# Two ends of a feed-forward pipeline: the last two weight groups summed by token halves, and two inner tiles begun on the first half alone

## The chip, the core and the metric

One NeuronCore of a Trainium2 chip runs the whole program. Its engines take instructions from queues of their own, in the order in which these were written: TensorE (PE, matmuls; PEld is its weight load), VectorE (DVE), ScalarE (ACT), GpSimd (POOL) and SyncE (SP, which here issues all DMAs). The metric is device microseconds (us) of one execution, the median of three runs.

## The reference

One layer of a streaming encoder on 1024 new frames and 64 sample frames, D = 1024:

```
h = x + 0.5 * post1(SwiGLU_1(pre1(x)))
h = h + post_mix(token_mix(pre_mix(h)))            # latent attention and stick-breaking attention
h = h + 0.5 * post2(SwiGLU_2(pre2(h)));  y = final(h)
SwiGLU(x) = (silu(x @ w_gate) * (x @ w_up)) @ w_down        # inner width 2816
pre1, post1, ..., final: y / sqrt(mean(y * y) + eps) * gain, over the 1024 features of a token
```

The change touches the two ends of this: pre1 with the first tiles of SwiGLU_1, and the last sums of SwiGLU_2 with post2, the residual and the final norm.

## The kernel before

**Layout.** Features lie on the 128 partitions (KT = 8 blocks of 128), tokens on the free axis. Tokens come in two groups: G1 of 576 (worked in halves of 288) and G2 of 512. Every operand is split into a high and a low part (`split`, lines 142 and 143: a cast on ACT, then a difference on DVE), and a product is three matmuls: high·high, high·low, low·high (`steps`).

**Feed-forward.** `ffn` is a generator that yields after each matmul, so that other stages can draw matmuls from it to fill PE. The inner width is 22 tiles of 128. For one tile it loads two units of `w_gate` and two of `w_up` (`unit`: a DMA of 128x512 into `wr`, four buffers; cast to `wh`, difference to `wl`, eight buffers each), and for each token chunk does 24 matmuls into a gate bank and 24 into an up bank (`f`, three PSUM banks), then the activation (lines 364 to 368) and the split into `hh` and `hl`. Four tiles make a group. A group's sum over its tiles with `w_down` (`down`) is issued after the first tile of the next group, and added into `y` on DVE (line 322). The groups are 4, 4, 4, 4, 4 and 2 tiles: tiles 20 and 21 are the last group, and `down_last` sums it. For the last `ffn` (second feed-forward, G2) it does so by token halves of 256.

**The start.** The 576 tokens of G1 are loaded and normed in two halves: eight squares on ACT, eight fp32 matmuls with ones on PE (`rms_pe`), Ln and Exp on ACT, then for each k a product with gain and r on DVE (line 266, into `t`), a cast to `xh` on ACT and a difference to `xl` on DVE. After the first half three matmuls are drawn from the `ffn`; the rest comes after the second half. The `ffn` takes tile 0 with both halves, then tile 1. After that `late` copies cached keys and values (`ks`, `vs`) from DRAM to DRAM, and the tokens of G2 (`p`) are loaded, squared and summed.

**The end.** `last` runs after the last sum: for each token half a norm, the residual (lines 279 and 280), a second norm, and the output (line 1106, two buffers of 256 KB, DMA at 1108).

**What sets the order.** The program is unrolled. A list scheduler then lays the instructions of each engine into one fixed order, by its own estimate of times; a waiting instruction holds all behind it in its queue.

Of the kernel before, what the change touches and what calls it, by code (L numbers as in the profile page):

```python
# [7 lines left out]
F32 = mybir.dt.float32  # L8
F32R = mybir.dt.float32r
AF = mybir.ActivationFunctionType  # L10
# [5 lines left out]
P = 128  # L16
# [37 lines left out]
EARLY = 3  # L54
# [15 lines left out]
class Layer:  # L70
# [232 lines left out]
    def ffn(self, pool, tmp, n, g, xhi, xlo, y, end=None, tail=None):  # L303
        nc, a = self.nc, self.a
        _, T, C = g
        wg, wu, wd = a[f"wg{n}"], a[f"wu{n}"], a[f"wd{n}"]
        pend = []

# [24 lines left out]
        def down_last(part, step, beside):  # L333
            ws = [[self.unit(pool, wd[mi][:, half * 512:half * 512 + 512]) for mi, _, _ in part] for half in range(2)]
            if step:
                order = [(dt, c0, step) for c0 in range(0, T, step) for dt in range(KT)]
            else:
                order = [(dt, c0, C) for dt in range(KT) for c0 in range(0, T, C)]
            for dt, c0, n in order:
                for _ in product(part, ws[dt // H], False, dt, c0, n):  # L340
                    yield True
                next(beside, None)

        for m in range(0, FT, GROUP):
            part = []
            for mi in range(m, min(m + GROUP, FT)):
                if mi == m + 1 and pend:
                    yield from down(pend.pop(0), m == GROUP)
                gw = units(wg[mi])
                uw = units(wu[mi])  # L350
                hh = pool.tile([P, T], F32R, name="hh")
                hl = pool.tile([P, T], F32R, name="hl")
                for c0 in range(0, T, C):
                    cs = slice(c0, c0 + C)
                    pg = self.bank_f()
                    pu = self.bank_f()
                    for ps, ws in ((pg, gw), (pu, uw)):
                        for k in range(KT):
                            wh, wl = ws[k // H]
                            ks = slice(k % H * P, k % H * P + P)  # L360
                            yield from self.steps(ps[:, :C], wh[:, ks], wl[:, ks], xhi[:, k, cs], xlo[:, k, cs],
                                                  k == 0, k == KT - 1)
                    s = tmp()[:, :C]
                    nc.scalar.activation(s, pg[:, :C], AF.Exp, scale=-1.0)
                    nc.scalar.activation(s, s, AF.Ln, bias=self.one)
                    nc.scalar.activation(s, s, AF.Exp, scale=-1.0)  # L366
                    nc.vector.tensor_tensor(s, pg[:, :C], s, op=ALU.mult)  # L367
                    nc.vector.tensor_tensor(s, pu[:, :C], s, op=ALU.mult)  # L368
                    self.split(hh[:, cs], hl[:, cs], x=s)
                part.append((mi, hh, hl))  # L370
            pend.append(part)
# [3 lines left out]
        yield from down_last(pend.pop(0), tail, end)  # L375
# [645 lines left out]
def body(tc, a, ctx):  # L1021
# [58 lines left out]
    def last(gi, y, res, pool, step):  # L1080

        t0, T, C = groups[gi]
        yT = a["yT"].rearrange("(k p) t -> p k t", p=P)
        for c0 in range(0, T, step):
            cs = slice(c0, c0 + step)
            tmp = lambda: pool.tile([P, step], F32, name="t", bufs=4)

            def norm():

                r = pool.tile([P, step], F32, name="r", bufs=4)  # L1090
                if c0 + step == T:
                    L.rms_pe(tmp, L.bank_f, [y[:, k, cs] for k in range(KT)], step, r)
                else:
                    for k in range(KT):
                        L.square(tmp, r, y[:, k, cs], k == 0)
                    L.rsqrt(L.bank_f, r, step, D, r)
                return r

            r = norm()
            for k in range(KT):  # L1100
                L.residual(res[:, k, cs], y[:, k, cs], "post2", k, r, None)
            r = norm()
            for k in range(0, KT, 2):
                o = pool.tile([P, 2, step], F32, name="out", bufs=2)
                for i in range(2):
                    nc.vector.scalar_tensor_tensor(o[:, i], y[:, k + i, cs], L.gain("final", k + i), r,
                                                   op0=ALU.mult, op1=ALU.mult)
                nc.sync.dma_start(yT[:, k:k + 2, t0 + c0:t0 + c0 + step], o)
# [17 lines left out]
    with tc.tile_pool(name="x0", bufs=1) as xp:  # L1126
# [4 lines left out]
        zero = L.ffn(F, fact, 1, G1, *x0, y0)  # L1131
        for c0 in (0, half):
# [6 lines left out]
            r = xp.tile([P, half], F32, name="r", bufs=2)  # L1139
            L.rms_pe(tmp, L.bank_f, [y[:, k, cs] for k in range(KT)], half, r)  # L1140
            L.at_r = 0.0
            L.scaled(tmp, lambda k: y[:, k, cs], "pre1", r, x0[0][:, :, cs], x0[1][:, :, cs], pace=False)

            if c0 == 0:
                for _ in range(EARLY):
                    next(zero)
# [167 lines left out]
```

## Time and profile before

| | us |
|---|---|
| median of three runs (2336.8 to 2340.3) | 2339.42 |
| the profiled execution, whole | 2337.27 |
| its span in the trace | 2335.5 |
| PE busy | 2256.7 (97%) |
| DVE busy | 1429.8 (61%) |
| ACT busy | 1287.3 (55%) |

PE is busy almost throughout; its slices of the span read 7 tenths in the first and 5 tenths in the last. A busy matmul counts from its start to its modelled end, so neighbours overlap; the rate is read from starts. A row of the timeline reads: start, busy us, engine, line, operation, output<-inputs, size, count, and in brackets the idle time before it and what ended it.

### The profile page before, as it was taken

What the parts mean: (1) busy time and instruction counts of PE and PEld (TensorE: products, weight loads), DVE (VectorE), ACT (ScalarE), POOL (GpSimd) and SP (SyncE); (2) the same over time, 40 slices, a digit from 0 to 9 for tenths busy, and PEclk for the clock granted to TensorE, in tenths of its full rate; (3) what the DMA queues carried; (4) which work ended last, traced back from release to release, by engine and by line L of the source; (5) the groups of instructions that cost most, each with busy time, mean ns of one, the idle gap of its engine ahead of it and who ended that gap; (6) DMA issues with size and microseconds to landing.
All of it is one profiled execution on the core that took longest, in us unless ns stands there. A gap on an engine that the chain in (4) does not pass through costs nothing.

```text
span 2335.5 us, 37504 instructions
## 1 busy us (share of the span) xinstructions
PE 2256.7 (97%) x13841; PEld 2034.3 (87%) x13841; DVE 1429.8 (61%) x2528; ACT 1287.3 (55%) x2494; POOL 32.9 (1%) x224
## 2 busy tenths in 40 slices
PE   7999999999999999999999999999999999999995
PEld 7999999989987877779888998999899898888884
DVE  5444444674348778755874377878777488444445
ACT  6443334463257878663553478777777445433333
POOL 0000000000000000000000000000000000000000
PEclk9999999999999999999999999999999999999998
DMA  6332222453454434343555532323222434333321
GB/s 211 102 96 81 84 78 86 143 183 119 167 155 128 139 98 128 108 140 99 162 159 181 162 96 88 102 73 100 73 73 70 135 106 147 121 96 96 98 86 36
DMA packets 186615, 268.80 MB, mean 115 GB/s; under 512 B 59216, under 2 KB 68048, under 8 KB 186400
## 3 DMA queue, kind: packets, MB, share of 16 engines
q1 hardware_dynamic: 186432, 266.41, 37.1%
q8 instruction: 109, 1.79, 0.3%
q14 instruction: 74, 0.61, 0.1%
HBM read 227.61 MB, written 40.88 MB: 115 GB/s over the span
## 4 chain that ended last, share of the span: by engine, by line
PE 73%; DVE 10%; ACT 8%; DMA 5%; issue 3%; SPq 1%; DVEq 0%; POOL 0%; ACTq 0%; POOLq 0%
PE f L157 50%; PE s L157 9%; PE t L157 6%; PE v L157 6%; DVE a L620 2%; PE t L161 2%; ACT a L615 1%; ACT a L614 1%; DVE a L617 1%; ACT a L616 1%; DMA e<-h 1%; DVE wl L143 1%; DVE pl L687 1%; DVE y L280 1%; ACT wh L142 1%
## 5 line engine op out<-in xcount | busy, mean ns | idle before, releaser
L157 PE MATMUL f<-xh,wh 128*128 128x288 f32 (+1 forms) x2112 | 695.2, 330 | 9.5 <-ACT xh L142 7.2
L157 PE MATMUL f<-xh,wl 128*128 128x288 f32 (+1 forms) x2112 | 695.9, 330 | 0.0
L157 PE MATMUL f<-xl,wh 128*128 128x288 f32 (+1 forms) x2112 | 694.9, 329 | 0.8 <-DVE xl L143 0.8
L142 ACT CAST wh<-wr 128x512 fp32r<-128x512 f32 x638 | 384.5, 619 | 495.7 <-PE f L157 341.0
L143 DVE TENSOR_TENSOR wl<-wr,wh 128x512 fp32r<-128x512 f32 x638 | 429.5, 688 | 246.6 <-ACT wh L142 223.8
L157 PEld LDWEIGHTS f<-xh,wh 128*128 128x128 f32 x2112 | 397.9, 189 | 40.1 <-ACT xh L142 8.3
L157 PEld LDWEIGHTS f<-xl,wh 128*128 128x128 f32 x2112 | 398.1, 189 | 29.8 <-DVE xl L143 1.7
L157 PEld LDWEIGHTS f<-xh,wl 128*128 128x128 f32 x2112 | 398.1, 188 | 29.2 <-issue 2.4
L157 PE MATMUL f<-hl,wh 128*128 128x288 f32 (+2 forms) x1072 | 351.6, 328 | 0.1
L157 PE MATMUL f<-hh,wh 128*128 128x288 f32 (+2 forms) x1072 | 349.9, 327 | 0.5 <-DVE y L322 0.3
L157 PE MATMUL f<-hh,wl 128*128 128x288 f32 (+2 forms) x1072 | 349.8, 326 | 0.0
L157 PEld LDWEIGHTS f<-hl,wh 128*128 128x128 f32 x1072 | 202.1, 189 | 14.6 <-issue 1.4
L157 PEld LDWEIGHTS f<-hh,wh 128*128 128x128 f32 x1072 | 201.7, 188 | 14.9 <-DVE y L322 1.3
L157 PEld LDWEIGHTS f<-hh,wl 128*128 128x128 f32 x1072 | 202.0, 188 | 13.9 <-issue 1.2
L322 DVE TENSOR_TENSOR y<-f,y 128x288 f32<-128x288 f32 (+2 forms) x248 | 127.7, 519 | 101.1 <-PE f L157 100.7
L367 DVE TENSOR_TENSOR act<-f,act 128x288 f32<-128x288 f32 (+1 forms) x132 | 70.2, 532 | 120.3 <-ACT act L366 120.0
L368 DVE TENSOR_TENSOR act<-f,act 128x288 f32<-128x288 f32 (+1 forms) x132 | 70.3, 533 | 76.3 <-PE f L157 72.9
L687 DVE TENSOR_TENSOR pl<-t,ph 128x384 fp32r<-128x384 f32 (+1 forms) x160 | 98.3, 631 | 25.0 <-ACT ph L686 23.7
L142 ACT CAST hh<-act 128x288 fp32r<-128x288 f32 (+1 forms) x132 | 65.1, 494 | 77.4 <-DVE act L368 77.1
L157 PE MATMUL v<-pl,v 128*128 128x256 f32 x320 | 89.8, 304 | 18.3 <-DVE pl L687 18.0
L686 ACT CAST ph<-t 128x384 fp32r<-128x384 f32 (+1 forms) x160 | 83.6, 542 | 29.4 <-PE t L161 27.7
L161 PE MATMUL t<-c_ident,a 128*128 128x128 f32 x616 | 90.5, 273 | 2.6 <-ACT a L631 2.6
(308 smaller groups left out, 3409.0 us busy)
## 6 DMA issues: line engine op xcount, KB each, us to landing
wr<-in_wg SPq DMA_DIRECT2D x176, 256.0 KB, 2.9
wr<-in_wu SPq DMA_DIRECT2D x176, 256.0 KB, 3.1
wr<-in_wd SPq DMA_DIRECT2D x176, 256.0 KB, 2.9
wr<-in_win SPq DMA_DIRECT2D x44, 256.0 KB, 3.1
kl<-ks SPq DMA_DIRECT2D x64, 128.0 KB, 2.8
wr<-in_wout SPq DMA_DIRECT2D x32, 256.0 KB, 2.9
h<-y SPq DMA_DIRECT2D x16, 288.0 KB, 2.5
p<-in_xT SPq DMA_DIRECT2D x16, 256.0 KB, 3.4
```

Of the source, the lines that this page charges most:

```text
L142: nc.scalar.copy(hi, x)
L143: nc.vector.tensor_tensor(lo, x, f(hi), op=ALU.subtract)
L157: self.nc.tensor.matmul(out, lhsT=lhsT, rhs=rhs, start=start, stop=stop)
L161: self.nc.tensor.transpose(out, x, ident)
L280: nc.vector.tensor_tensor(y, y, x, op=ALU.add)
L322: nc.vector.tensor_tensor(yy, ps[:, :C], yy, op=ALU.add)
L367: nc.vector.tensor_tensor(s, pg[:, :C], s, op=ALU.mult)
L368: nc.vector.tensor_tensor(s, pu[:, :C], s, op=ALU.mult)
L614: nc.scalar.activation(av, z, AF.Abs)
L620: nc.vector.tensor_tensor_scan(a[:, 0:n - 1][:, ::-1], zs[:, 1:n][:, ::-1], a[:, 0:n - 1][:, ::-1], BIG, op0=ALU.add, op1=ALU.subtract)
L686: nc.scalar.copy(ph[:, end:], tr[:, end:])
L687: nc.vector.tensor_tensor(pl[:, end:], tr[:, end:], f(ph[:, end:]), op=ALU.subtract)
```

## The change

- At the start, the first half's squares are summed on DVE (line 221), and one matmul with ones gives the sum. `ffn` gets `lead`: the first two inner tiles do their 48 matmuls each for the first token half before either does its second half. Matmuls are drawn between the steps of the second half's norm and split.
- At the end, the sum of group 16 to 19 is no longer issued between tiles 20 and 21: `down_last` sums all six tiles, 16 to 21, for the first token half and then for the second, and after every product one step of `last` is issued. `last` is now a generator: first half's norm, residual, second norm and the squares of the second half lie between the products.
- The twelve `w_down` units which this needs at once have room in `spare`: nine lie in the place of the group-1 input `x`, three in `wh` and `wl`. The last `hh` and `hl` lie in another pool. The output buffers are five instead of two (`e`).

```diff
-    def ffn(self, pool, tmp, n, g, xhi, xlo, y, end=None, tail=None):
+    def ffn(self, pool, tmp, n, g, xhi, xlo, y, end=None, tail=None, spare=None, own=None, lead=0):
...
+        def unit(src):
+            if not room:
+                return self.unit(pool, src)
+            hi, lo = room.pop(0)
+            raw = pool.tile([P, 512], F32, name="wr")
+            nc.sync.dma_start(raw, src)
+            self.split(hi, lo, x=raw)
+            return hi, lo
...
+        for c0 in range(0, T, C) if lead else ():
+            for mi in range(lead):
+                if c0 == 0:
+                    ahead.append(open_tile(mi))
+                yield from inner(*ahead[mi], c0)
+        part.extend((t[0], t[3], t[4]) for t in ahead)
         for m in range(0, FT, GROUP):
+            for mi in range(m, min(m + GROUP, FT)):
+                if mi == m + 1 and pend and not (tail and m + GROUP >= FT):
+                    yield from down(pend.pop(0), m == GROUP)
...
+        if spare:
+            room.extend(spare())
-        yield from down_last(pend.pop(0), tail, end)
+        yield from down_last(sum(pend, []), tail, end)
...
+        one, two = slice(0, step), slice(step, T)
+        r1, r2, r3, r4 = row(), row(), row(), row()
+        for k in range(KT):
+            L.square(tmp, r1, y[:, k, one], k == 0)
+            yield
+        ps = None
+        for k in range(KT):
+            if k < KT - 1:
+                L.square(tmp, r3, y[:, k, two], k == 0)
+            if k == 0:
+                L.rsqrt(L.bank_f, r1, step, D, r1)
+            elif k < 5:
+                for i in range(2 * k - 2, 2 * k):
+                    moved(i, one, r1)
+                    L.square(tmp, r2, y[:, i, one], i == 0)
+            elif k == 6:
+                L.rsqrt(L.bank_f, r2, step, D, r2)
+            if k < KT - 1:
+                yield
+        sq = tmp()
+        nc.scalar.activation(sq, y[:, KT - 1, two], AF.Square)
...
+        scale(ps, r3)
+        for k in range(0, KT, 2):
+            out(k, one, r2)
+        for k in range(KT):
+            moved(k, two, r3)
+        L.rms_pe(tmp, L.bank_f, [y[:, k, two] for k in range(KT)], step, r4)
+        for k in range(0, KT, 2):
+            out(k, two, r4)
...
-        zero = L.ffn(F, fact, 1, G1, *x0, y0)
+        zero = L.ffn(F, fact, 1, G1, *x0, y0, lead=LEAD)
...
+            if c0 == 0:
+                for k in range(KT):
+                    L.square(tmp, r, y[:, k, cs], k == 0)
+                L.rsqrt(L.bank_f, r, half, D, r)
+                L.scaled(tmp, lambda k: y[:, k, cs], "pre1", r, x0[0][:, :, cs], x0[1][:, :, cs], pace=False)
+                for _ in range(3 * KT):
+                    next(zero)
+                continue
             L.rms_pe(tmp, L.bank_f, [y[:, k, cs] for k in range(KT)], half, r)
-            if c0 == 0:
-                for _ in range(EARLY):
+            for _ in range(3 * KT):
+                next(zero)
+            for k in range(KT):
+                L.scaled(tmp, lambda k: y[:, k, cs], "pre1", r, x0[0][:, :, cs], x0[1][:, :, cs], ks=[k], pace=False)
+                for _ in range((LEAD - 1) * 6 if k < KT - 1 else 0):
                     next(zero)
```

What this does to the queues is seen at three places. SP at the start of the program, first before, then after the change (`ks` and `vs` are the DRAM copies, `p` the tokens of G2, `wr` weights):

```order
L299 DMA wr<-in_wu 128x512 x2
L299 DMA wr<-in_wg 128x512
L129 DMA ks_88<-in_c_k 16x16384
L299 DMA wr<-in_wg 128x512
L299 DMA wr<-in_wu 128x512
L130 DMA vs_94<-in_c_v 16x16384
L299 DMA wr<-in_wu 128x512
L1050 DMA p<-in_xT 128x512 x3
```

```order
L299 DMA wr<-in_wg 128x512 x2
L129 DMA ks_88<-in_c_k 16x16384
L130 DMA vs_94<-in_c_v 16x16384
L1081 DMA p<-in_xT 128x512
L299 DMA wr<-in_wu 128x512 x2
L1081 DMA p<-in_xT 128x512 x4
```

The two copies now stand one behind the other, and the first `p` directly behind them.

ACT at the start, where the second token half is cast to `xh`, before and after (`act` is an activation of tile 0 or 1, `hh` its cast):

```order
L142 CAST xh<-t 128x288
L366 ACTIVATE act<-act 128x288
L142 CAST xh<-t 128x288 x5
L217 ACTIVATE p<-p 128x512
L142 CAST wh<-wr 128x512
L142 CAST xh<-t 128x288 x2
L220 ACTIVATE p<-p 128x512
```

```order
L243 ACTIVATE r<-f,eps 128x288
L244 ACTIVATE r<-r 128x288
L142 CAST xh<-t 128x288 x2
L217 ACTIVATE p<-p 128x512
L142 CAST xh<-t 128x288 x2
L142 CAST hh<-act 128x288
L220 ACTIVATE p<-p 128x512
L142 CAST xh<-t 128x288 x3
L374 ACTIVATE act<-f 128x288
L375 ACTIVATE act<-act,ones 128x288
L220 ACTIVATE p<-p 128x512
L142 CAST xh<-t 128x288
```

Before, one square of `p` stands ahead of the last two casts; now one stands ahead of the last six, a second ahead of four and a third ahead of the last.

DVE at the end of the program, from the last sums on, before and after (`y<-f,y` adds a product, lines 279 and 280 are the residual, `r<-r,t` adds squares, 1106 and 1130 are the output):

```order
L322 TENSOR_TENSOR y<-f,y 128x256 x6
L279 SCALAR_TENSOR_TENSOR y<-y,c_gains,r 128x256 x2
L280 TENSOR_TENSOR y<-y,h 128x256 x2
...
L221 TENSOR_TENSOR r<-r,t 128x256 x7
L1106 SCALAR_TENSOR_TENSOR out<-y,c_gains,r 128x256 x8
L279 SCALAR_TENSOR_TENSOR y<-y,c_gains,r 128x256 x2
```

```order
L221 TENSOR_TENSOR r<-r,t 128x256 x3
L279 SCALAR_TENSOR_TENSOR y<-y,c_gains,r 128x256
L334 TENSOR_TENSOR y<-f,y 128x256
L280 TENSOR_TENSOR y<-y,h 128x256
L221 TENSOR_TENSOR r<-r,t 128x256 x2
L334 TENSOR_TENSOR y<-f,y 128x256
L221 TENSOR_TENSOR r<-r,t 128x256
L1130 SCALAR_TENSOR_TENSOR e<-y,c_gains,r 128x256 x3
L334 TENSOR_TENSOR y<-f,y 128x256
L1130 SCALAR_TENSOR_TENSOR e<-y,c_gains,r 128x256 x5
L279 SCALAR_TENSOR_TENSOR y<-y,c_gains,r 128x256 x2
```

The residual and squares of the first half now stand among the sums of the second; the first half's output stands around the last sum.

## Rows read from the trace of the kernel before

**Rows 1.** Stages: length, busy PE, PEld, DVE, ACT, POOL (count), PE clock, DMA share, GB/s.

```profile
13.50:39.70 26.20, 21.00 (x98) 18.03 (x98) 17.97 (x41) 15.94 (x38) 0.00 (x0) 0.80 0.60 197
39.70:80.00 40.30, 40.30 (x307) 40.30 (x306) 21.55 (x40) 22.05 (x46) 0.00 (x0) 1.00 0.41 126
80.00:2255.30 2175.30, 2132.39 (x13150) 1925.17 (x13149) 1342.70 (x2340) 1216.67 (x2342) 32.68 (x220) 1.00 0.38 115
2255.30:2288.00 32.70, 32.70 (x146) 27.09 (x145) 13.34 (x20) 8.18 (x13) 0.00 (x0) 1.00 0.15 47
2301.00:2335.50 34.50, 11.18 (x36) 7.56 (x34) 21.82 (x56) 12.99 (x32) 0.00 (x0) 0.77 0.18 61
```

**Rows 2.** Chain of waits, start of the program: start us, us, what.

```profile
27.28 7.25 DMA p<-in_xT
...
36.07 8.94 PE f L157 x54
```

**Rows 3.** Timeline of ACT, where the second token half is normed and cast.

```profile
26.05 0.45 ACT L244 ACTIVATE r<-r 128x288 f32<-128x288 f32 x1
...
29.76 1.29 ACT L142 CAST xh<-t 128x288 fp32r<-128x288 f32 x3 [0.99 <-DVE t L266]
34.55 0.63 ACT L217 ACTIVATE p<-p 128x512 f32<-128x512 f32 x1 [3.50 <-DMA p<-in_xT]
```

**Rows 4.** Timeline of SP, the two copies from DRAM to DRAM.

```profile
21.11 0.50 SPq L129 DMA_DIRECT2D ks<-in_c_k  x1
...
25.40 0.71 SPq L130 DMA_DIRECT2D vs<-in_c_v  x1
```

**Rows 5.** DMA issues of the first 45 us: count, us from issue to landing.

```profile
ks<-in_c_k SPq DMA_DIRECT2D x1, 8.1
vs<-in_c_v SPq DMA_DIRECT2D x1, 7.8
```

**Rows 6.** Timeline of PE: tile 21, then the last sums, at a steady rate.

```profile
2283.64 0.39 PE L157 MATMUL f<-xh,wl 128*128 128x512 f32 x1
...
2287.72 0.39 PE L157 MATMUL f<-xh,wl 128*128 128x512 f32 x1
...
2293.90 0.28 PE L157 MATMUL f<-hh,wh 128*128 128x256 f32 x1
...
2300.62 0.28 PE L157 MATMUL f<-hh,wl 128*128 128x256 f32 x1
```

**Rows 7.** Chain of waits from the last sum to the end.

```profile
2302.33 0.88 DVE y L279 x2
...
2308.27 0.35 DVE r L221
...
2311.83 6.34 PE f L157 x18
2318.19 0.48 ACT r L243
2319.15 0.88 DVE y L279 x2
```

**Rows 8.** Timeline of DVE in the same stretch.

```profile
2300.22 0.42 DVE L322 TENSOR_TENSOR y<-f,y 128x256 f32<-128x256 f32 x1 [0.29 <-PE f L157]
...
2308.17 3.60 DVE L221 TENSOR_TENSOR r<-r,t 128x256 f32<-128x256 f32 x7
...
2330.63 1.67 DVE L1106 SCALAR_TENSOR_TENSOR out<-y,c_gains,r 128x256 f32<-128x256 f32 x4 [1.51 <-DMA out_yT<-out]
```

**Rows 9.** Timeline of SP: loads of `w_down` ahead of the last two sums.

```profile
2226.74 19.54 SPq L299 DMA_DIRECT2D wr<-in_wd  x8
...
2265.49 2.89 SPq L299 DMA_DIRECT2D wr<-in_wd  x4
```

**Rows 10.** Page: a costly group (count, busy us, mean ns), a DMA issue (us to landing).

```profile
L142 ACT CAST wh<-wr 128x512 fp32r<-128x512 f32 x638 | 384.5, 619 | 495.7 <-PE f L157 341.0
...
wr<-in_wd SPq DMA_DIRECT2D x176, 256.0 KB, 2.9
```

More of the change, by code (lines that the diff above doesn't have):

```diff
@@ L50 @@
 SLACK = 1.15
-EARLY = 3
+LEAD = 2
 EASE = 0.8
@@ L333, in down_last @@
         def down_last(part, step, beside):
[L334 to L340, printed above, removed]
+            ws = [[unit(wd[mi][:, half * 512:half * 512 + 512]) for mi, _, _ in part] for half in range(2)]
@@ L341, in down_last @@
+            order = [(dt, c0) for c0 in range(0, T, step) for dt in range(KT)] if step else \
+                [(dt, c0) for dt in range(KT) for c0 in range(0, T, C)]
+            for dt, c0 in order:
+                for _ in product(part, ws[dt // H], False, dt, c0, step or C):
                     yield True
                 next(beside, None)
-        for m in range(0, FT, GROUP):
-            part = []
[L346 to L371, printed above, removed]
@@ new lines, in open_tile, with inner @@
+        def open_tile(mi):
+            gw = units(wg[mi])
+            uw = units(wu[mi])
+            room = own if own and mi == FT - 1 else pool
+            hh = room.tile([P, T], F32R, name="hh")
+            hl = room.tile([P, T], F32R, name="hl")
+            return mi, gw, uw, hh, hl
+        def inner(mi, gw, uw, hh, hl, c0):
+            cs = slice(c0, c0 + C)
+            pg = self.bank_f()
+            pu = self.bank_f()
+            for ps, ws in ((pg, gw), (pu, uw)):
+                for k in range(KT):
+                    wh, wl = ws[k // H]
+                    ks = slice(k % H * P, k % H * P + P)
+                    yield from self.steps(ps[:, :C], wh[:, ks], wl[:, ks], xhi[:, k, cs], xlo[:, k, cs],
+                                          k == 0, k == KT - 1)
+            s = tmp()[:, :C]
+            nc.scalar.activation(s, pg[:, :C], AF.Exp, scale=-1.0)
+            nc.scalar.activation(s, s, AF.Ln, bias=self.one)
+            nc.scalar.activation(s, s, AF.Exp, scale=-1.0)
+            nc.vector.tensor_tensor(s, pg[:, :C], s, op=ALU.mult)
+            nc.vector.tensor_tensor(s, pu[:, :C], s, op=ALU.mult)
+            self.split(hh[:, cs], hl[:, cs], x=s)
@@ L1078, in finish, with last @@
             t = L.done(t + SLACK * (T / 960 + 0.15))
-    def last(gi, y, res, pool, step):
+    def last(gi, y, res, pool):
         t0, T, C = groups[gi]
+        step = T // 2
         yT = a["yT"].rearrange("(k p) t -> p k t", p=P)
[L1084 to L1108, printed above, removed]
@@ new lines, in last, with scale, moved, out @@
+        tmp = lambda: pool.tile([P, step], F32, name="t", bufs=4)
+        row = lambda: pool.tile([P, step], F32, name="r", bufs=4)
+        def scale(ps, r):
+            nc.scalar.activation(r, ps, AF.Ln, bias=L.eps, scale=1.0 / D)
+            nc.scalar.activation(r, r, AF.Exp, scale=-0.5)
+        def moved(k, cs, r):
+            L.residual(res[:, k, cs], y[:, k, cs], "post2", k, r, None)
+        def out(k, cs, r):
+            o = pool.tile([P, 2, step], F32, name="e", bufs=5)
+            for i in range(2):
+                nc.vector.scalar_tensor_tensor(o[:, i], y[:, k + i, cs], L.gain("final", k + i), r,
+                                               op0=ALU.mult, op1=ALU.mult)
+            nc.sync.dma_start(yT[:, k:k + 2, t0 + cs.start:t0 + cs.stop], o)
@@ new lines, in last @@
+        sq = tmp()
+        nc.scalar.activation(sq, y[:, KT - 1, two], AF.Square)
+        ps = L.bank_f()[:, :step]
+        L.mul(ps, lhsT=L.ones, rhs=r3, start=True, stop=False)
+        L.mul(ps, lhsT=L.ones, rhs=sq, start=False, stop=True)
+        scale(ps, r3)
[6 more added lines that the diff above has]
+            out(k, two, r4)
@@ L1208, in body @@
     x3 = pair(lp, T2, "x")
-    tmp = lambda: lp.tile([P, T2], F32, name="e", bufs=3)
+    tmp = lambda: lp.tile([P, T2], F32, name="e", bufs=5)
     L.wait(L.at_r)
@@ L1218, in body, with spare @@
     y3 = lp.tile([P, KT, T2], F32, name="y")
-    third = L.ffn(F, fact, 2, G2, *x3, y3, tail=T2 // 2)
+    def spare():
+        both = [z.rearrange("p k t -> p (k t)") for z in pair(fp, T1, "x")]
+        return [[z[:, i:i + 512] for z in both] for i in range(0, KT * T1, 512)]
+    third = L.ffn(F, fact, 2, G2, *x3, y3, end=lambda: last(1, y3, h, lp), tail=T2 // 2, spare=spare, own=lp)
     L.filler = third
```

16 lines of the change are left out of this document (13 added, 3 removed).

## The prediction

> **What bounds the kernel now.** I read the table of stages first, since a mean over the span says little here. From 39.7 to 2288 PE is busy without gaps worth the name (40.30 of 40.30, 2132 of 2175, 32.70 of 32.70 [rows 1]); the change leaves the matmuls of that stretch and their order nearly as they were, and I count it as unchanged. Two stretches are not bound by PE: 13.5 to 39.7, where the granted clock is 0.80 and PE has done only 82 matmuls of the feed-forward (98 records less 16 passes of the norm's eight ones matmuls), and 2301.0 to 2335.5, 34.5 us in which the norms of the two token halves run one after the other and PE is busy for 11 [rows 1].
>
> At the start I then read the chain of waits. Its longest link is not the norm but a transfer: `p`, issued at 27.28, lands 7.25 later, and PE resumes at 36.07 [rows 2]. The ACT timeline says why PE cares: a square of `p` sits in ACT's queue ahead of the last two casts of the second token half and holds ACT for 3.50 us [rows 3]. At the end the chain has DVE nearly alone: residual from 2302.33, squares from 2308.27, then eighteen ones passes and the second half's whole tail from 2318.19 [rows 7].
>
> **The change at the end, step by step.** Rates first: 18 steps from 2283.64 to 2287.72 are 0.2267 us per 512-wide matmul, 56 steps from 2293.90 to 2300.62 are 0.120 per 256-wide one [rows 6].
>
> - Both versions are alike up to the end of tile 20's products. Counting back from 2287.95 (2287.72 + 0.23), where the last sums begin, 96 + 48 matmuls of 0.2267 put that at 2255.3.
> - After the change: tile 21, 48 × 0.2267 = 10.9. Then 16 products of six tiles, 288 × 0.120 = 34.6. (The four moved tiles cost 192 × 0.120 − 96 × 0.2267 = 1.3 more in halves.)
> - Tile 21's split must be done before its matmuls. Before, the last sums took 2287.95 to 2300.74 (2300.62 + 0.12) for 96 × 0.12 = 11.5, so 1.3 was lost there. Now five other tiles stand ahead of it in the first product, 1.8 us of work: I take 0.5 (bounds 0 and 1.3).
> - Two ones matmuls for r1 and r2 now stand between products. Nine of them took 6.34 at the end, at a clock of 0.77, so 0.7 each [rows 1, 7]; on a busy PE less: 0.5 each, 1.0 (bounds 0.6 and 1.4).
> - The second ones matmul waits for DVE, with the last product behind it on PE. r1 is ready 0.5 + 0.48 + 0.42 after the tenth product begins, with latencies 1.5 [rows 3, 7]. From there DVE has eight residual pairs (2302.33 to 2308.27, 5.9), twelve adds at 0.35 to 0.51 (the first of the chain; 3.60 for seven), and five sums at 0.42 [rows 7, 8]: 12.2 to 14.1, so done at 13.7 to 15.6. PE gets there after six products, 13.0. A wait of 0.7 to 2.6; I take 1.0, near the lower end, because the adds now alternate between two accumulators instead of chaining on one.
>
> PE is then through at 2255.3 + 10.9 + 34.6 + 0.5 + 1.0 + 1.0 = 2303.3, where before it was at 2301. Behind that hangs one sum (0.42), one square (taken as 0.42 too), a ones matmul (0.5), Ln (0.48) and Exp (0.42, a little under the 0.45 of 288 columns) and some 0.5 of latencies: the second half's residual begins at 2306.1 instead of 2319.15 [rows 3, 7, 8]. From there to the end of the span it was 16.35; 1.5 goes, since the third of the half's four output pieces need no longer wait for a buffer (1.51 [rows 8]), and 14.85 stays. End at 2320.95 instead of 2335.5: **14.5 us saved**. With each bound at its worst (0.8, 0.4, 1.6, and the 1.5 kept) it is 10.2, at its best 16.4. What the first half's squares, residual and output cost DVE and ACT is hidden by the second half's 17.3 us of matmuls (144 × 0.12); without that cover they would cost the 17 us that they cost now.
>
> Here a page of the Trainium skill would say otherwise. In the steady row 256 columns take 0.120 [rows 6]. "TensorE: Matmul & The Clock Gate", section "Back-to-back issue gap", gives N/2.4 + 2.5 ns, 109 ns for 256 columns. By it the 288 matmuls are an estimated 31.4 and the end comes 3 us sooner; the row is this very stream, so I stay with it.
>
> **The change at the start.** At 39.70 PE has done 82 of the 192 matmuls of tiles 0 and 1 and goes on at 40.3/307 = 0.131 each [rows 1], so 120 are done at 44.7. After the change these 120 are: both tiles for the first half (96), and tile 0's gate for the second.
>
> - First half: its norm loses seven ones matmuls on PE and gains seven adds on DVE; but the weight casts now stand ahead of Ln on ACT. I count nothing for it (−0.5 to +1). The second half's r is ready at 26.5 [rows 3]; now, with two more units of weights split earlier, I take 25 (bounds 24 and 26.5).
> - PE's 72 matmuls behind the second half's ones cover 72 × 0.131 = 9.5 us; the ones end a Ln and an Exp before r, at 24, so to about 33.5. The sixth cast ended at 31.05, 4.5 after r [rows 3]; eight at that pace are through by 31, PE would not wait at all, and 120 would be done at 33.5 + 24 × 0.131 = 36.7: 8.0 saved. That is one bound.
> - But ACT's queue has the first `p` square after two casts, the second after four, the third before the eighth. `p` now follows both copies directly on SP. `ks` landed at 21.1 + 8.1 = 29.2, `vs` at 25.4 + 7.8 = 33.2, `p` behind it at 34.5 [rows 2, 4, 5]. With `ks` issued at about 20.8 (the weights ahead of it are split a little earlier than for the 21.1), `vs` at its heels and `p` at 22, `p` lands no earlier than 22 + 7.25 = 29.3 and no later than 28.9 + 4.0 + 1.3 = 34.2. I take 33, nearer the later end, since the row of `p` had only the rest of one copy ahead of it.
> - From 33: square 0.63, two casts, `hh`, the second `p` (about 35), square, three casts that wait for DVE products, two activations, third square, last cast at 39, and two adds of `p` on DVE ahead of its difference: tile 0's second gate ends at about 40, 4.7 before the 44.7. In pieces it keeps PE half idle, so the lower clock may last some us past it, as in the stage with 0.80 before; I take off 0.5. **4.2 us saved**, bounds 0 and 8.0.
>
> The second place for the skill: the row shows `p` 7.25 us underway with one copy in front. "DMA: Bandwidth & Descriptors", section "Queues, rings and completion order", says that an SDMA engine consumes descriptors in ring order, so `p` would wait for all of both copies. By that rule the landing is near 34 and the gain 3.2; by the flat 7.25 it is near 29 and the gain about 7.
>
> **Sum.** 2337.27 − 14.5 − 4.2 = 2318.6 for the profiled execution; it lay 2.15 under the median, so 2320.7 against 2339.42. I say 2320.5.
>
> **Rivals.**
>
> - *Late `p` (0.15).* The start gives nothing: `p` lands at 38 or later, or the third one does, and ACT sits ahead of the casts as before. For it: the 3.50 us wait that is there already, and three squares instead of one among the casts. Against it: 9.5 us of matmuls that need none of this. 2337.27 − 14.5 + 2.15 = 2324.9.
> - *Early `p` (0.08).* It lands near 29 and the casts are never held: 8.0 at the start, some 15 at the end: 2316.4.
> - *DVE bounds the second half (0.10).* Adds at 0.51 and each switch between sums, squares and residual paying its latency: PE waits 2.6 or more before the last product, the end gives 10.2: 2337.27 − 10.2 − 4.2 + 2.15 = 2325.0. For it: DVE is already at 21.8 of 34.5 in the tail [rows 1], and its work is now pressed beside the sums.
> - *The weights come late (0.04; the other side).* Place: the first product over six tiles, which needs six units, and the fifth, which needs the other six; all twelve pass SP, ACT and DVE during tiles 20 and 21, 21.8 us. Four units took 2.89, 0.72 each; eight took 19.54, 2.44 each, but those waited for PE to free `wh` [rows 9], which nine of the twelve need not. At 0.72 they are hidden; at 2.44, 29.3, they come 7.5 late and the time is 2328. It is slower than before from (21.8 + 18.7)/12 = 3.4 us per unit. If each went its round alone (2.9 to landing, 0.62 for the cast [rows 10], as much for the difference: 4.1), 49.2 − 21.8 = 27.4 are lost and the time is 2348. Against it: four buffers keep loads in flight, and DMA is at 0.15 there [rows 1].
>
> **How the numbers follow.** My forecast, 2317 to 2324, has 0.62; with the rivals 0.99, and 0.01 is for what I did not think of. The range 2313 to 2328 holds the first three rivals and leaves out the last one's far end. 0.2%, 4.7 us, is about what a measurement here can tell from no change. Faster than that needs more than 4.7 of the 18.7: all cases but the late weights, 0.94. Within it 0.02, slower 0.04.
>
> **What would show it.** In the trace after: sums of 256 columns at 0.120 without gaps to about 2299 of a span near 2317, less than 20 us from the last of them to the end; one wait of about 1 us of PE for DVE before the last product; no wait for `w_down`; residual of the second half beginning some 15 us before the end. At the start ACT waiting for `p` between the second and third cast of the second half, PE pausing after about 33 and running on at about 40. Wrong if PE pauses in the sums for a weight or a bank, if the tail is over 22 us, or if `p` lands before 30 or after 36.

## The result: 1.05% faster, and the profile after

Median of four runs each: 2339.84 us before (2336.8 to 2340.3), 2315.18 after (2311.39 to 2316.89); ratio 0.9895, 95% interval 0.9878 to 0.9912, so between 20.6 and 28.5 us are saved. The forecast was 2320.5 (2313 to 2328): the time lies in that range, but below the 2317 to 2324 to which the forecast gave 0.62 of its chances.

The profiled execution of the changed kernel took 2316.89, with a span of 2315.1: 20.4 us shorter than the span of before. The medians lie 24.7 apart because the one execution is 2.57 under its median and the other 1.71 over it. The longer runs of the changed kernel have the lower granted clock: the two of 2316.9 and 2316.7 had a mean of 0.996, those of 2313.7 and 2311.4 one of 0.998, and 0.002 of 2315 are 4.6 us. So single steps are read below from positions in the trace, not from differences of medians.

The table of stages of the changed kernel answers to [rows 1]; columns as there. The last sums now begin at 2261.34.

```profile
13.50:39.70 26.20, 24.36 (x145) 22.29 (x146) 17.43 (x41) 16.13 (x40) 0.00 (x0) 1.00 0.61 195
39.70:80.00 40.30, 40.30 (x306) 40.30 (x305) 22.18 (x42) 22.63 (x48) 0.00 (x0) 1.00 0.41 132
2261.30:2297.30 36.00, 35.82 (x293) 35.38 (x293) 21.32 (x55) 10.79 (x28) 0.00 (x0) 1.00 0.01 2
2300.30:2315.10 14.80, 5.45 (x16) 3.93 (x16) 9.19 (x24) 3.91 (x11) 0.00 (x0) 0.78 0.32 106
```

At the start 145 records of matmuls stand where there were 98, and the clock reads 1.00 where it was 0.80. The 1.00 does not hold for all of it: from 14 to 17.9 matmuls start 0.24 us apart, the pace of 1.2 GHz, where 0.131 is the pace later. PE's timeline of after:

```profile
17.41 0.44 PE L157 MATMUL f<-xh,wh 128*128 128x288 f32 x1
17.65 0.44 PE L157 MATMUL f<-xl,wh 128*128 128x288 f32 x1
```

Before, there was a second stretch at 0.24, from 36.07 to 39.55, right behind PE's wait of 3.73 us for a cast. In this execution of after there is none. At the end 34.5 us of norms behind the last sum have become 18, the last 14.8 of which are the second half's tail.

**Where the 20.4 us come from.** The same instruction, ACT's first activation of a gate, shows how far the two executions are apart. First the timeline of before, then that of after, at tile 3 and at tile 18 of the last feed-forward.

```profile
77.25 0.40 ACT L364 ACTIVATE act<-f 128x288 f32<-128x288 f32 x1
...
2228.61 0.59 ACT L364 ACTIVATE act<-f 128x512 f32<-128x512 f32 x1
```

```profile
70.86 0.40 ACT L374 ACTIVATE act<-f 128x288 f32<-128x288 f32 x1
...
2223.76 0.59 ACT L374 ACTIVATE act<-f 128x512 f32<-128x512 f32 x1
```

6.4 us are saved by 77 us of the span; 4.85 are left at 2228; so the end saves 20.4 − 4.85 = 15.55, and the middle gave back 1.5. The change has no step of its own there. Three stretches of the middle have a lower granted clock after, and two before; each costs some (1 − 0.83) × 10 = 1.7 us of full clock, so the one more is about the size of the 1.5. But PE's waits there are not the same either (they add up to 42.3 us after and 41.1 before), and between 77 and 2228 the distance goes up to 7.1 and down to 3.8 us. What the 1.5 is made of is not shown. One stretch of after:

```profile
1640.00:1650.00 10.00, 8.81 (x53) 8.52 (x54) 6.98 (x12) 6.75 (x12) 0.44 (x3) 0.83 0.11 42
```

**The start after.** ACT's timeline, where the second half is cast, answers to [rows 3]:

```profile
23.53 0.44 ACT L244 ACTIVATE r<-r 128x288 f32<-128x288 f32 x1
24.56 0.86 ACT L142 CAST xh<-t 128x288 fp32r<-128x288 f32 x2 [0.59 <-DVE t L266]
31.09 0.63 ACT L217 ACTIVATE p<-p 128x512 f32<-128x512 f32 x1 [5.67 <-DMA p<-in_xT]
31.63 0.75 ACT L142 CAST xh<-t 128x288 fp32r<-128x288 f32 x2
...
33.26 0.63 ACT L220 ACTIVATE p<-p 128x512 f32<-128x512 f32 x1 [0.54 <-DMA p<-in_xT]
...
36.34 0.41 ACT L142 CAST xh<-t 128x288 fp32r<-128x288 f32 x1
```

The casts stop for 5.67 us at the first square of `p`, as forecast. SP's timeline and the landings of the two copies (count, us) say why; they answer to [rows 4, 5]:

```profile
19.89 0.50 SPq L129 DMA_DIRECT2D ks<-in_c_k  x1
20.45 0.58 SPq L130 DMA_DIRECT2D vs<-in_c_v  x1
21.07 0.61 SPq L1081 DMA_DIRECT2D p<-in_xT  x1
```

```profile
ks<-in_c_k SPq DMA_DIRECT2D x1, 6.4
vs<-in_c_v SPq DMA_DIRECT2D x1, 8.6
```

`ks` is there at 26.3, `vs` at 29.05, `p` at 31.09. PE's timeline shows what that costs: the 24th, 96th and 120th matmul of tiles 0 and 1 are these, and the last three wait for the last cast.

```profile
19.76 0.29 PE L157 MATMUL f<-xh,wl 128*128 128x288 f32 x1
...
32.14 0.29 PE L157 MATMUL f<-xh,wl 128*128 128x288 f32 x1
...
36.80 0.40 PE L157 MATMUL f<-xh,wh 128*128 128x288 f32 x1 [0.50 <-ACT xh L142]
37.92 0.40 PE L157 MATMUL f<-xl,wh 128*128 128x288 f32 x1 [0.71 <-DVE xl L143]
38.16 0.29 PE L157 MATMUL f<-xh,wl 128*128 128x288 f32 x1
```

The 120 are done at 38.3. Without a pause they would be done at 32.27 + 24 × 0.131 = 35.4, so the pause costs 2.9.

**The end after.** PE's timeline: the first of the last sums, the two ones matmuls between them, the last sum.

```profile
2261.34 0.28 PE L157 MATMUL f<-hh,xh 128*128 128x256 f32 x1
...
2280.93 0.59 PE L157 MATMUL f<-r,ones 128*128 128x256 f32 x2
...
2294.65 0.70 PE L157 MATMUL f<-r,ones 128*128 128x256 f32 x2 [0.18 <-DVE r L221]
...
2297.21 0.28 PE L157 MATMUL f<-hh,wl 128*128 128x256 f32 x1
```

The chain of waits behind it (start, us, what) answers to [rows 7]:

```profile
2297.82 0.34 DVE y L334
...
2298.65 0.71 PE f L157 x2
...
2299.39 0.48 ACT r L1121
...
2300.34 0.88 DVE y L279 x2
...
2307.67 0.48 ACT r L243
...
2309.51 2.38 DVE e L1130 x6
```

No gap stands in the sums but the 0.18 (0.34 from start to start beyond the pitch). The residual of the second half begins 14.76 us before the end.

### The profile page after: what moved, and what is told of

Same layout as the page of the kernel before. It is cut to its first block, busy times and chain, and to the rows that moved or that the text cites. A ratio compares the mean times of both kernels' runs of the same rounds, so it can differ in the third digit from the quotient of the medians.

```text
span 2315.1 us, 37626 instructions
## 1 busy us (share of the span) xinstructions
PE 2246.7 (97%) x13911; PEld 2032.5 (88%) x13911; DVE 1427.7 (62%) x2533; ACT 1285.0 (56%) x2494; POOL 32.9 (1%) x224
## 4 chain that ended last, share of the span: by engine, by line
PE 73%; DVE 10%; ACT 8%; DMA 4%; issue 3%; SPq 1%; DVEq 0%; POOL 0%; ACTq 0%; POOLq 0%
PE f L157 50%; PE s L157 9%; PE t L157 7%; PE v L157 6%; DVE a L651 2%; PE t L161 2%; DVE a L648 1%; ACT a L647 1%; ACT a L646 1%; ACT a L645 1%; DVE pl L718 1%; DVE wl L143 1%; ACT wh L142 1%; DMA tmp<-in_xT 1%; DVE a L657 1%
## 5 line engine op out<-in xcount | busy, mean ns | idle before, releaser
L142 ACT CAST wh<-wr 128x512 fp32r<-128x512 f32 x629 | 378.7, 619 | 467.8 <-PE f L157 309.8
L143 DVE TENSOR_TENSOR wl<-wr,wh 128x512 fp32r<-128x512 f32 x629 | 422.8, 687 | 250.5 <-ACT wh L142 228.2
L157 PEld LDWEIGHTS f<-xh,wl 128*128 128x128 f32 x2112 | 398.5, 189 | 29.3 <-issue 2.4
L157 PE MATMUL f<-hl,wh 128*128 128x288 f32 (+2 forms) x1032 | 336.2, 326 | 0.0
L157 PE MATMUL f<-hh,wh 128*128 128x288 f32 (+2 forms) x1032 | 334.5, 325 | 1.1 <-DVE y L334 1.1
L157 PE MATMUL f<-hh,wl 128*128 128x288 f32 (+2 forms) x1032 | 334.5, 324 | 0.0
L157 PEld LDWEIGHTS f<-hh,wh 128*128 128x128 f32 x1032 | 193.7, 188 | 13.7 <-DVE y L334 1.7
L157 PEld LDWEIGHTS f<-hl,wh 128*128 128x128 f32 x1032 | 193.9, 188 | 12.9 <-issue 1.4
L157 PEld LDWEIGHTS f<-hh,wl 128*128 128x128 f32 x1032 | 193.9, 188 | 12.6 <-issue 1.2
L334 DVE TENSOR_TENSOR y<-f,y 128x288 f32<-128x288 f32 (+2 forms) x240 | 121.9, 512 | 96.5 <-PE f L157 96.1
L718 DVE TENSOR_TENSOR pl<-t,ph 128x384 fp32r<-128x384 f32 (+1 forms) x160 | 98.2, 630 | 24.5 <-ACT ph L717 23.2
```

The source lines that it names most:

```text
L142: nc.scalar.copy(hi, x)
L143: nc.vector.tensor_tensor(lo, x, f(hi), op=ALU.subtract)
L157: self.nc.tensor.matmul(out, lhsT=lhsT, rhs=rhs, start=start, stop=stop)
L334: nc.vector.tensor_tensor(yy, ps[:, :C], yy, op=ALU.add)
L718: nc.vector.tensor_tensor(pl[:, end:], tr[:, end:], f(ph[:, end:]), op=ALU.subtract)
```

## Experiments

All times are medians beside runs of the kernel before on the same chip, there 2338.3 to 2338.4 (13 to 17 runs).

**Start and end apart.** The end alone:

```
-        zero = L.ffn(F, fact, 1, G1, *x0, y0, lead=LEAD)
+        zero = L.ffn(F, fact, 1, G1, *x0, y0)        # and the start loop of before, EARLY = 3
```

> The start of the kernel before with the end of the changed one. Theory A (the two parts are worth what the two traces show, and add up): the end alone saves 15.6 us: tile 21's last matmul to the first ones matmul of r3 36.0 us, the second half's residual 3.0 us after that, 14.8 us from there to the end of the span; 2339.8 - 15.6 = 2324.2 us, between 2322.5 and 2326.5. Theory B (the forecast's own terms for the end were right, and what the changed kernel gained beyond them came from elsewhere): 14.5 us, 2325.3 us, with PE waiting about 1 us for DVE before the last product. Theory C (the start and the end are not independent, a part of the 24.7 us is only there with both): less than 13 us saved, above 2327 us.

Measured: 2321.36 (ratio 0.9932, 0.9916 to 0.9947): 15.9 us by the ratio. The end is worth what it is in the changed kernel: from the first of the last sums (2265.61) to the end of the span (2319.4) it is 53.8, as in the changed kernel (2315.1 − 2261.34 = 53.8). The start alone:

```
-                if mi == m + 1 and pend and not (tail and m + GROUP >= FT):
+                if mi == m + 1 and pend:             # and last(), tail, spare, own as before
```

> The start of the changed kernel with the end of the kernel before. Theory A (parts add up): 120 matmuls of tiles 0 and 1 are done at 38.3 us of the span instead of 44.7, so 6.4 us saved, less what low clock in the middle gives or takes (up to 3 us between runs): 2333.4 us, between 2331 and 2336. Theory B (the forecast's 4.2 us for the start): 2335.6 us. Theory C (the start's gain is lost again in the middle, where other work waits for other things): within 2 us of 2339.8.

Measured: 2333.2 (0.9977, 0.9966 to 0.9988), 5.4 us (2.8 to 8.0); 120 matmuls are done at 39.5. 15.9 and 5.4 make 21.3, inside the interval of the whole change: no sign that the parts depend on each other, and the end is some three quarters of the gain. The median can't tell theory A's 6.4 for the start from theory B's 4.2. The trace is nearer to B: the gate of tile 3 that stands at 77.25 before and at 70.86 after is here at 73.17, so 4.1 are saved by then.

**Cover at the end.**

```
                 for _ in product(part, ws[dt // H], False, dt, c0, step or C):
                     yield True
-                next(beside, None)
```

> The changed kernel, with no step of the norms issued between the products of the last six tiles: all of it comes behind the last sum. Theory A (what saved the time at the end is that the first half's norms lie beside the second half's matmuls): PE is through the sums about 1.4 us sooner, but then residual of the first half 5.9, some fifteen adds at 0.34, a second norm of about 2 and eight outputs of 0.41 stand ahead of the second half's residual, which begins 13.5 us later than in the changed kernel: 2328.7 us (2326 to 2332). Theory B (the gain came from the six-tile sum itself, from the tile order or from the five output buffers): not more than 5 us slower, under 2320 us.

Measured: 2330.76 (0.9968, 0.9957 to 0.9978). PE's timeline shows where the time went, behind the last sum at 2294.72:

```profile
2306.40 1.22 PE L157 MATMUL f<-r,ones 128*128 128x256 f32 x2 [10.97 <-DVE r L221]
```

From the first sum (2260.14) to the second half's residual (2311.79) it is 51.65, in the changed kernel 39.0: 12.65 more, 13.5 expected. Of the 7.5 us that are left by the ratio the start has 5.4, so some 2 are left for the six-tile sum and the five buffers, less than these intervals can show; what saves is that the norms lie beside matmuls.

**DVE's slack there.**

```
+        idle = pool.tile([P, step], F32, name="idle")
...
                     L.square(tmp, r2, y[:, i, one], i == 0)
+                    nc.vector.tensor_tensor(idle, r2, r2, op=ALU.add)
```

> The changed kernel, with eight further adds of 128x256 on DVE, into a tile that nobody reads, one behind each square of the first half's second norm. Theory A (DVE is just done when PE comes to the second ones matmul, no slack is left there): eight adds of 0.34 are 2.7 us, PE waits about 2.5 to 3 us for DVE ahead of the last product instead of 0.3, and the end comes 2.5 us later: 2317.7 us. Theory B (DVE has slack between the products, idle 0.77 at a time): the adds vanish in it, PE's wait stays under 1 us, 2315 us.

Measured: 2321.46 (0.9929, 0.9910 to 0.9948). PE's wait grew as theory A has it:

```profile
2299.34 0.48 PE L157 MATMUL f<-r,ones 128*128 128x256 f32 x1 [2.23 <-DVE r L221]
...
2306.56 6.61 PE L157 MATMUL f<-t,ones 128*128 128x256 f32 x16 [2.71 <-ACT t L241]
```

First sum (2263.98) to the second half's residual (2304.85) is 40.9, in the changed kernel 39.0: 1.9 more for some 2.7 of adds (8 × 0.34). First sum to end (2320.6) is 56.6, 2.9 more; the other 1.0 lies in the tail, where the sixteen ones passes took 6.61 us instead of 5.57. The median is higher by more than that; its runs have a mean clock of 0.994 to 0.995 where the changed kernel's had 0.996 to 0.998, which is some 4 us. The forecast's place where DVE decides is right, and the changed kernel has less than 1 us of slack there.

**Two output buffers.**

```
-            o = pool.tile([P, 2, step], F32, name="e", bufs=5)
+            o = pool.tile([P, 2, step], F32, name="out", bufs=2)
...
-    tmp = lambda: lp.tile([P, T2], F32, name="e", bufs=5)      # the tiles that shared `e`
+    tmp = lambda: lp.tile([P, T2], F32, name="e", bufs=4)
```

> The changed kernel with two output buffers instead of five. Theory A (the forecast's 1.5 us for the buffers): DVE waits for an output transfer once in each half, and from the first of the last sums to the end of the span it is 55.3 us or more instead of 53.8; 2316.7 us. Theory B (the transfers are over before the buffer is wanted, or the wait lies beside other work): 53.8 us, 2315.2.

Measured: 2321.24 (0.9934, 0.9919 to 0.9949); first sum (2264.30) to end (2321.4) 57.1, 3.3 more. DVE's timeline has both waits:

```profile
2302.71 0.88 DVE L1130 SCALAR_TENSOR_TENSOR out<-y,c_gains,r 128x256 f32<-128x256 f32 x2 [1.20 <-DMA out_yT<-out]
...
2316.48 0.88 DVE L1130 SCALAR_TENSOR_TENSOR out<-y,c_gains,r 128x256 f32<-128x256 f32 x2 [1.51 <-DMA out_yT<-out]
```

The forecast counted the second. The first half's outputs now stand in DVE's queue around the second half's residual, so there a buffer is waited for as well. The two waits are 2.7 of the 3.3; the sixteen ones passes of the tail, 6.28 us instead of 5.57, are the rest. To the old order the buffers would be worth the 1.5 of [rows 8], which no run here tests.

**One tile ahead.**

```
-LEAD = 2
+LEAD = 1
```

> The changed kernel with one inner tile ahead instead of two (LEAD = 1): 48 fewer matmuls stand between the second half's ones and the first matmul that needs its casts. Theory A (the start gains by the matmuls that cover the second half's norm and casts): PE has 24 matmuls, 3.1 us, of cover left where 72 covered 9.4; it then waits for casts that p still holds until about 37, and 120 matmuls are done at about 44 instead of 38.3: 2321 us, the start's gain nearly gone. Theory B (the gain is the first half's sum on DVE and the full clock, the number of tiles ahead matters little): 120 done before 41, 2317 us or less.

Measured: 2321.45 (0.9932, 0.9910 to 0.9955); PE waits 5.4 us at once for a cast of `xh`, and 120 matmuls are done at 43.6. Theory A. The table of stages shows the clock going with it:

```profile
13.50:39.70 26.20, 20.65 (x107) 18.91 (x107) 16.35 (x38) 15.55 (x38) 0.00 (x0) 0.87 0.55 179
```

**`p` without the copies ahead of it.** In the changed kernel, and then in the kernel before:

```
-        nc.sync.dma_start(self.ks[2], a["c_k"])
-        nc.sync.dma_start(self.vs[2], a["c_v"])
...
         L.scaled(tmp, get, "pre1", r, *x1)
+        for z, src in ((L.ks[2], a["c_k"]), (L.vs[2], a["c_v"])):
+            nc.sync.dma_start(z[0:1, 0:8], f(x1[0])[0:1, 0, 0:8])
+            nc.sync.dma_start(z, src)
```

> The changed kernel, with the two DRAM copies ks and vs made to wait for the last cast of x of the second token group (two 32-byte writes stand ahead of them), so that nothing of them lies ahead of p. Theory A (p was late because the two copies lay ahead of it on the queue, and the late p held the casts of the second token half): p lands within 4 us of its issue, by about 25 us; the casts of the second half run through by about 31; PE runs without pause behind the ones matmuls, 96 matmuls done at 32.3 and 120 at 35.4 instead of 38.3: 2.9 us less than the changed kernel, 2312.3 us. Rival B (a load of p takes 7 us whatever lies ahead): p lands at about 28, the first cast of the second half, which now stands behind the first square of p, is held until 28.4, and 120 matmuls are done at 38 or later: no gain, 2315 us or more.

> The kernel before, with nothing changed but the two DRAM copies, which wait for the second group's x as in the run on the changed kernel. Theory A (late p held the casts of the kernel before by 3.5 us, and without that they end sooner): p lands by 28, the last cast of the second half at about 33 instead of 36, 120 matmuls done at about 41.5 instead of 44.7: up to 3 us saved by 77 us of the span, half of what the new start saves; in the time 2336 us, less what the copies cost later (2.4 us in the other run). Theory B (PE waits for the second half's norm anyway, p or no p): 120 done at 44 or later, 2338 us or more.

Measured: 2314.37 (0.9908, 0.9893 to 0.9922) and 2337.17 (0.9993, 0.9982 to 1.0004): no time that can be told from the kernel without the edit. Yet at the start theory A holds in both traces. In the changed kernel `p`, issued at 20.74, is squared at 24.62 without a wait; from the 24th matmul to the 120th it is 15.6 instead of 18.4 us in the changed kernel, and 15.4 instead of 19.65 in the one before. In the changed kernel this is given back when the copies come, at 105: 2.2 us ahead of the changed kernel at 81, the edited one is 0.75 behind it from 136 on. PE's timeline there:

```profile
121.26 0.40 PE L157 MATMUL f<-xh,wh 128*128 128x288 f32 x1 [1.31 <-DVE act L377]
...
129.02 0.40 PE L157 MATMUL f<-xh,wh 128*128 128x288 f32 x1 [1.13 <-DVE act L377]
```

In the kernel before, one wait of 2.08 us for ACT (line 320) at 109.7 and a lower clock right behind it, 0.83 from 110 to 120, take back most of it; that the copies cause this wait is not shown. Theory A of the first run, 2312.3 us, is not confirmed: in the changed kernel the copies cost at their new place about what they cost at the old one.

**The copies on ACT's DMA queue**, at the same late place:

```
-            nc.sync.dma_start(z, src)
+            nc.scalar.dma_start(z, src)
```

> As the run with the two DRAM copies made to wait for the second group's x, but issued from ACT's DMA queue instead of SP's. There the copies, issued at 105, held what stood behind them on SP, and PE waited twice, 1.31 and 1.13 us, for DVE at 121 and 129. Theory A (a queue works its transfers off in order, so only what stands behind a copy on its own queue is late): both waits are gone, and the 2.2 us gained by tile 3 are still there at 160 us. Theory B (the copies fill the DMA engines themselves, whatever queue they come from): the waits stay, within 0.5 us of their size.

Measured: 2313.99 (0.9907, 0.9890 to 0.9923). PE's timeline has both waits still:

```profile
119.55 0.40 PE L157 MATMUL f<-xh,wh 128*128 128x288 f32 x1 [0.83 <-DVE act L377]
...
126.94 0.40 PE L157 MATMUL f<-xh,wh 128*128 128x288 f32 x1 [0.77 <-DVE act L377]
```

They shrank by 0.48 and 0.36. Theory A failed, and by its own measure, within 0.5 us, theory B held, if barely: from one execution of each, a third of the cost (1.6 together, from 2.4) went with SP's queue and two thirds stay from ACT's too.

**`p`'s squares on POOL**, the copies as they were:

```
+    def square_pool(self, tmp, acc, x, first):
+        to = acc if first else tmp()
+        self.nc.gpsimd.tensor_tensor(to, x, x, op=ALU.mult)
+        if not first:
+            self.nc.gpsimd.tensor_tensor(acc, acc, to, op=ALU.add)
...
-        r = L.rms(tmp, L.bank_f, (get(k) for k in range(KT)), T2, D)
+        r = L.rms(tmp, L.bank_f, (get(k) for k in range(KT)), T2, D, square=L.square_pool)
```

> The changed kernel, with the squares of p and their sum done on POOL instead of ACT and DVE; the copies stay where they are. Theory A (what costs is only that squares of p stand in ACT's queue ahead of the casts): p still lands at about 31, but no cast waits for it; 120 matmuls are done at about 35.4 instead of 38.3, 2.9 us less than the changed kernel, 2312.3 us. Rival B (the casts are held by ACT's or DVE's own work or by the late weights, not by p): PE still pauses between 33.9 and 38, no gain. Rival C: POOL slows DVE beside it, and the sum of p comes so late that PE waits for x of the second token group: slower than the changed kernel.

Measured: 2316.27 (0.9902, 0.9886 to 0.9918). `p` comes late as before (31.6), no cast waits, and from the 24th to the 120th matmul it is 15.6. Late `p` costs nothing when its square is not in ACT's queue, and the square there costs nothing when `p` is early: only both together cost. The 24th matmul came 1.0 us later than in the changed kernel, so 120 were done at 36.5. The time forecast by theory A, 2312.3, is not confirmed: 2.8 us is less than these medians can show.

**What the pause costs beside its length.** Four other kernels of this section have the changed start with its pause: the start alone, no cover, the added adds, two buffers. At the gate of tile 3 they are 4.1, 5.1, 4.0 and 2.9 us ahead of the kernel before, where the changed kernel is 6.4 ahead; 0.3 to 1.3 of the difference is there at the 24th matmul already. In three of the four, all but the one without cover, the matmuls behind the pause start 0.24 apart, until 42 to 45. The table of stages from 40 to 50, in the changed kernel and then with two buffers:

```profile
40.00:50.00 10.00, 10.00 (x78) 10.00 (x77) 7.57 (x14) 7.46 (x17) 0.00 (x0) 1.00 0.60 192
```

```profile
40.00:50.00 10.00, 10.00 (x60) 10.00 (x60) 7.75 (x14) 7.76 (x17) 0.00 (x0) 0.76 0.59 184
```

In the runs without the pause (copies later, on ACT's queue, squares on POOL) the clock reads 1.00 from 30 to 50, and they are 8.6, 9.8 and 7.4 ahead at that gate. So the 6.4 of the changed kernel's trace is the best of five; their mean is 4.5. Why the clock fell behind the pause in three executions and not in the other two is not shown.

**The second half's sum on DVE too**, on top of that, and then with its ones matmul 24 matmuls later:

```
-            L.rms_pe(tmp, L.bank_f, [y[:, k, cs] for k in range(KT)], half, r)
+            for k in range(KT):
+                L.square(tmp, r, y[:, k, cs], k == 0)
+            L.rsqrt(L.bank_f, r, half, D, r)         # second run: behind the 24 next(zero)
```

> The changed kernel with the squares of p and their sum on POOL (as before in this study) and with the second token half's squares summed on DVE too, as the first half's are, so that one ones matmul stands on PE instead of eight. Theory A (PE's 2.7 us of ones matmuls are on its path, and the 9.4 us of matmuls behind them cover a later r): 120 matmuls are done about 2.3 us sooner than with POOL alone, at about 34 instead of 36.4, and the time is 2.3 us less than there and some 4 less than the changed kernel: 2311 us. Theory B (r comes later by seven adds on DVE, the casts with it, and PE waits for them instead): 120 done at 36 or later, 2314 us or more.

> As the run before it with both sums taken off ACT and PE (p's squares on POOL, the second half's squares summed on DVE), but its one ones matmul now stands behind 24 more matmuls of the feed-forward on PE. Theory A (there PE waited 3.98 us only because the ones matmul stood at the head of its queue before DVE had the sum; what matters is where a waiting instruction stands): PE comes to it at about 23.7, waits 1 us or less, the casts of the second half are through by about 33.4, no low clock follows, and 120 matmuls are done by about 35 instead of 40.0 there and 36.4 with POOL alone: 2313 us or less. Theory B (PE waits again, for r's casts behind it, since only 48 matmuls are left as cover): 120 done after 37, no better than the changed kernel.

Measured: 2317.29 (0.9916, 0.9900 to 0.9931) and 2316.47 (0.9911, 0.9895 to 0.9927). Theory A fell twice: 120 matmuls were done at 40.1 and 39.1. PE's timeline of the one, then of the other:

```profile
24.58 0.85 PE L157 MATMUL f<-r,ones 128*128 128x288 f32 x1 [3.98 <-DVE r L221]
```

```profile
24.50 1.33 PE L157 MATMUL f<-r,ones 128*128 128x288 f32 x2 [3.31 <-DVE r L221]
```

DVE had the sum at 24.5 in both, since its adds stand between differences of weights, and PE, once its matmuls ran out, waited 3.3 or 4.0 us for one instruction, where in the changed kernel the last six of the eight took 2.7 (19.89 to 22.58). The second guess (1 us or less) took PE's arrival for 23.7; it came at 21.2, and the clock reads 0.67 from 20 to 30, where no low clock was expected. No variant is shown to be faster than the changed kernel.

## Why the forecast held

By its own steps; the mechanism came out at both ends, and the sizes less well than the sum of the steps makes it look. By the number alone the rival *early p*, 2316.4, is nearer to 2315.18 than the forecast, but it is not what happened: `p` landed at 31.1 and the casts were held for 5.67 us.

- *Tile 21 and the last sums, 10.9 + 34.6.* Right. The sums begin at 2261.34, which is 2255.3 − 4.85 + 10.9, and run at 0.120. The 3 us less that the forecast weighed rest on a misreading. The section of the Trainium skill, "TensorE: Matmul & The Clock Gate", "Back-to-back issue gap", calls N/2.4 + 2.5 ns the gap of an isolated matmul; for a stream of weight loads and matmuls it gives 131 ns at 512 columns. The rows here do not agree with that either (226.7 ns at 512 [rows 6]), and the row decided rightly.
- *Wait for tile 21's split, 0.5.* Nothing: no gap in the first product.
- *Two ones matmuls, 1.0.* From 2261.34 to 2297.33 are 35.99: 34.56, 0.34 of waiting and so 1.1 for the two.
- *DVE's wait, 1.0.* 0.34, and the place was right. From the first residual (2282.68) to the last add before the ones matmul (2294.6) DVE took 11.9 us, where 12.2 to 14.1 were counted: the adds run at some 0.34 each (two in 0.67), just under the 0.35 to 0.51. Eight adds more make the wait 2.2, near the 2.6 of the rival that DVE bounds the second half. The best case of 16.4 for the end counts this wait as nothing, though its own lower bound was 0.7; by the bounds it is 15.7.
- *From the last sum to the residual, 2.8; tail 14.85.* 3.0 and 14.76.
- *The end, 14.5.* 15.55, by 0.5 and 0.7 of the waits above. The cover that this rests on is shown: without it 12.65 of them are lost, not the 17 that the forecast named.
- *The start, 4.2.* 6.4 in this execution, 2.9 to 5.1 in the four others with this start. The chain of events was the forecast one: r at 24 (25), casts stopped by `p`, PE pausing at 33.9, on again at 37.9 (33.5 and 40). Two sizes were off. `p` landed at 31.1, not 33: `ks` took 6.4 us, not 8.1 [rows 5], and `vs` 8.6 from 20.45. And the 0.5 taken off for a lower clock was not lost here: behind PE's pauses it stayed at 1.00. That was luck, since in three of the four others it fell; there the term is too small.
- *Ring order.* `vs` landed at 29.05 and `p` 2 us behind it, 10 after its issue, where it takes 3.9 at most with no copy ahead. So the rule of the Trainium skill, "DMA: Bandwidth & Descriptors", section "Queues, rings and completion order", that descriptors are consumed in ring order, was the nearer of the two; it put the landing near 34 because it took the copies for slower than they were here. The trace agrees that `p` came after both copies; that the order of the ring and not the copies' load held it is not shown.
- *Middle, 0.* −1.5 in these two executions; its cause is open, as said above.
- *Weights late.* Nine loads of `w_down` pass SP in 11.55 us, the other three soon after, and the last cast ends at 2251.6, 9.7 before the sums: hidden, as forecast. SP's timeline answers to [rows 9]:

```profile
2232.78 11.55 SPq L317 DMA_DIRECT2D wr<-in_wd  x9
2245.95 2.00 SPq L299 DMA_DIRECT2D wr<-in_wd  x3
```

Sum: 14.5 + 4.2 = 18.7 was forecast and 15.55 + 6.4 − 1.5 = 20.4 measured in the two profiled executions. The rest of the 24.7 is the two profiled executions' places among the runs.

## What to carry to other kernels

Behind the last matmul look for work on half of the data that can lie beside the other half's matmuls: here that is worth 13 us of the 15.5. A transfer that nobody waits for can hold one that somebody does: look at what stands ahead of a late load on its own queue, and look for its price where it is moved to; here it came back. Where an instruction of a later stage stands in an in-order queue mattered more here than how long it takes: squares of 0.63 us held the casts for 5.67. And one trace is one draw: the same start was worth 2.9 to 6.4 us in five executions, so read a small step from several.

## What was not expected of the hardware

POOL's squares, 1.0 to 1.6 us each, doubled DVE's differences beside them. The costliest groups of DVE in that run, first from 34 to 52 us, with POOL busy, then from 60 to 100, without:

```profile
L143 DVE TENSOR_TENSOR wl<-wr,wh 128x512 fp32r<-128x512 f32 x8 | 11.1, 1399 | 3.2 <-ACT wh L142 3.1
...
L383 DVE TENSOR_TENSOR act<-f,act 128x288 f32<-128x288 f32 x2 | 0.9, 446 | 0.0
```

```profile
L143 DVE TENSOR_TENSOR wl<-wr,wh 128x512 fp32r<-128x512 f32 x13 | 8.8, 692 | 14.0 <-ACT wh L142 13.7
...
L383 DVE TENSOR_TENSOR act<-f,act 128x288 f32<-128x288 f32 x4 | 1.8, 458 | 7.5 <-ACT act L382 7.5
```

1399 ns against 692 for the operation with two inputs in SBUF, and no change for the one that reads a PSUM bank (446 against 458). The Trainium skill, "SBUF — State Buffer", section "Who interferes with whom", says that a DVE instruction with two SBUF inputs contends with a POOL instruction that reads SBUF; these rows agree.

The clock can be lower behind a wait. In the run with one ones matmul behind DVE's sum, PE idled 3.98 us and then went at 0.24 per matmul, at 1.2 GHz, until 29.3, before it was back at 0.131; the stretch from 20 to 30 reads 0.66:

```profile
20.00:30.00 10.00, 5.95 (x24) 5.43 (x25) 7.53 (x19) 5.20 (x14) 0.00 (x0) 0.66 0.90 306
```
